# A first norm's rows loaded late, and a weight ring of 44 rows in place of 42

## The chip, the cores and the metric

The kernel runs on one core of a Trainium2 chip. The metric is the device time of one execution in microseconds (us). Engines are TensorE (PE in the profile; PEld is its weight load), VectorE (DVE), ScalarE (ACT), GpSimd (POOL) and SyncE (SP), which here issues nearly all DMA transfers.

## The reference

One decoder layer over 256 tokens of width 1024, all in float32:

```python
h = token_mixer(x, w_in, g_sb, g_dil, w_out, rel_bias)   # 8 stick-breaking and 8 dilated heads of 64
x = layer_norm(ALPHA * x + h, ln1_g, ln1_b)
h = grouped_moe(x, w_router, b_router, w_gate, w_up, w_down)
x = layer_norm(ALPHA * x + h, ln2_g, ln2_b)

# grouped_moe: 16 experts in 4 groups; each token picks one group, in it its top 2
for e in range(16):
    hid = silu(t @ w_gate[e]) * (t @ w_up[e])
    y = y + gate_dense[:, e:e+1] * (hid @ w_down[e])      # each w is 1024 x 1024
```

The expert weights are 16 x 3 x 4 MB, 201 MB, and each is used once.

## The kernel before

**The ring.** Each expert matrix is cut into 8 rows of 128 x 1024 floats (512 KB); `seq` lists the 384 rows in the order of use: gate, up and down of expert 0, then of expert 1, and so on. SBUF holds them in slots: `slot(i)` with i below `BIG` = 8 has room for 4 rows, the others for 2. `SMALL` slots of two rows (8 and 9) come from the base pool, which is there from the start, `LATE` of them (10, 11, 12) from a pool that is opened when attention is over. That makes a ring of 42 rows. Three more places take two rows each once and are not refilled: `fourth`, the slot `YS` (which afterwards is `ys2`, the experts' outputs and the gathered tokens), and the slot `OT` (attention's output before, and afterwards `acc`, the sum that the last norm reads). `lead` says which of the first 48 rows go where, `todo` is the list of the others in pairs.

**Refills.** When the last row of a slot has been multiplied, `taken` calls `load_next`, which takes the next pairs of `todo` into the slot (L236; `load_rows` splits a load where the rows go on in another matrix). The loads are issued by SP in program order, so a load that waits for its slot holds up those behind it. Slots 0 to 5 hold attention's input weights first, 6 and 7 the output projection. The last matrix, expert 15's down, is loaded by columns (L209). In expert 6 some slots are not refilled at once: they are `held` for a branch that recomputes experts with too many tokens, and refilled behind it, in expert 7.

**The experts.** They go in pairs; `pairs()` writes TensorE's order out by hand. Per expert: 16 rows of gate and up (L258), the activation (ACT L716, DVE L721), transposes (L723), 8 rows of down (L733). In between stand the gather of the next pair's tokens (L639, copied by ACT into `ys2[:, 1]`, then L648) and the spread of the last pair's outputs into `acc` (L670, L672), whose first is at row 2 of expert 2. The order on the other engines is the scheduler's.

**The first norm.** `xs` holds the normalised tokens without gain and bias. `ln1` holds gain and bias of the first norm as rows on all 128 partitions: loaded and broadcast at the start by `ln_rows` (L263, L264), the bias multiplied by ALPHA (L300). `residual()` is called when expert 0's down is done and writes ALPHA * (xs * gain + bias) into `acc`, with DVE (L679) and POOL (L680).

Of the kernel before, what the change touches and what calls it, by code (L numbers as in the profile page):

```python
# [13 lines left out]
F32 = mybir.dt.float32  # L14
I32 = mybir.dt.int32
AF = mybir.ActivationFunctionType
ALU = mybir.AluOpType
AX = mybir.AxisListType

D = 1024  # L20
T = 256
NT = T // 128
# [11 lines left out]
ALPHA = 2.0 ** 0.25  # L34
# [39 lines left out]

BIG = 8
W_IN = 6
SMALL, LATE = 2, 3
LATER = 40
CHUNKS = ((0, 512, 2), (512, 768, 4), (768, 1024, 2))
BANKS = {"mm": 3, "z": 2, "tr": 1, "om": 2}  # L80
SPARE = 6
# [3 lines left out]
def trunk(ctx: ExitStack, tc: tile.TileContext, x, w_in, g_sb, g_dil, w_out, ln1_g, ln1_b, ln2_g, ln2_b,  # L85
          rel_bias, w_router, b_router, w_gate, w_up, w_down, cst_d, rou_d, att_d, out):
    nc = tc.nc
# [4 lines left out]
    def pool(stack, name, bufs=1, **kw):  # L92
        return stack.enter_context(tc.tile_pool(name=name, bufs=bufs, reuse_waits="tile", **kw))

    base = pool(ctx, "base")
# [3 lines left out]
    def bank(name):  # L99
        return ps.tile([128, 512], F32, name=name, bufs=BANKS[name])  # L100
# [7 lines left out]
    OT, YS = BIG + SMALL + LATE, BIG + SMALL + LATE + 1  # L108
# [4 lines left out]
    def slot(i):  # L113
        p = base if i < BIG + SMALL or i == OT else late[0]
        return p.tile([128, room(i), D], F32, name=f"s{i}")

    def load_win(i, col, parts=(4, 4), between={}):
        src = w_in[:, col:col + 512].rearrange("(j p) f -> p j f", j=8)
        w = slot(i).rearrange("p a b -> p (a b)").rearrange("p (j f) -> p j f", j=8)
        j = 0  # L120
        for n in parts:
            if j in between:
                between[j]()
            nc.sync.dma_start(w[:, j:j + n], src[:, j:j + n])
            j += n
        return lambda j: w[:, j]
# [8 lines left out]
    xs = base.tile([128, NT, D], F32, name="xs")  # L135
# [13 lines left out]
    eps_rms = cst[:, C_EPS:C_EPS + 1]  # L149
    eps_ln = cst[:, C_EPS + 1:C_EPS + 2]  # L150
    ln_col = base.tile([128, 2, 8], F32, name="ln_col")
    ln1 = base.tile([128, 2, D], F32, name="ln1")
    pos1 = base.tile([128, NT, E], F32, name="pos1")
    gate = base.tile([128, NT, E], F32, name="gate")
    gate_ov = base.tile([128, NT, E], F32, name="gate_ov")
# [28 lines left out]
    def gathered(xp):  # L184
        xg = by_model()
        for j in range(8):
# [3 lines left out]

    seq = [(e, m, j) for e in range(E) for m in range(3) for j in range(8)]
    lead = {BIG: (0, 2), BIG + 1: (2, 4), BIG + 2: (4, 6), None: (6, 8), BIG + 3: (8, 10), BIG + 4: (10, 12),
            0: (12, 16), 1: (16, 20), YS: (20, 22), OT: (22, 24),
            **{i: (4 * i + 16, 4 * i + 20) for i in range(2, BIG)}}
    todo = [seq[n:n + 2] for n in range(48, len(seq), 2)]

    todo[-4:] = [[(E - 1, 2, q)] for q in range(4)]
    order = []
# [49 lines left out]
    def taken(row, refill=True):  # L248
        i = ring.pop(row)[1]
        if refill and i is not None and i < OT:  # L250
            load_next(i)
        return i

    def widened(p, row, xg, i):
        w = ring[row][0].rearrange("p (q c r) -> p c q r", c=2, r=4)
        j = row[2]
        for c in range(2):
            nc.tensor.matmul(p[c * CAP:(c + 1) * CAP], xg[:, j, i * CAP:(i + 1) * CAP], w[:, c],  # L258
                             start=j == 0, stop=j == 7)

    def ln_rows(dst, g, b):
        for i, v in enumerate((g, b)):
            nc.gpsimd.dma_start(dst[0:1, i], v)  # L263
            nc.gpsimd.partition_broadcast(dst[:, i], dst[0:1, i])  # L264


    with ExitStack() as mix:
# [11 lines left out]
        with ExitStack() as att:  # L279
# [16 lines left out]
            nc.sync.dma_start(ln_col[:, 0], ln1_g.rearrange("o (p j) -> (o p) j", j=8))  # L296
            nc.sync.dma_start(ln_col[:, 1], ln1_b.rearrange("o (p j) -> (o p) j", j=8))
            nc.sync.dma_start(rou, rou_d)
            ln_rows(ln1, ln1_g, ln1_b)
            nc.vector.tensor_scalar(ln1[:, 1], ln1[:, 1], ALPHA, None, op0=ALU.mult)  # L300
            c_vd, c_qd, c_kd = [load_win(i, c) for i, c in ((3, 2560), (4, 1536), (5, 2048))]
            wo = []
            for i in range(W_IN, BIG):
# [160 lines left out]
        for i, w in enumerate((wg, wr)):  # L464
            nc.vector.tensor_tensor(w, wr, gT[:, HG * (i + 1):HG * (i + 2)][:, :, None].to_broadcast([128, 8, E]),
                                    op=ALU.mult)
# [24 lines left out]
        for t in range(NT):  # L491
# [32 lines left out]
            if t == NT - 1:  # L524
# [41 lines left out]
                                           op0=ALU.is_ge, op1=ALU.mult)  # L566
# [3 lines left out]
                                           op0=ALU.is_equal, op1=ALU.mult)  # L570
# [10 lines left out]
            with tc.high_priority(offset=-LATER):  # L581
                if not t:
# [6 lines left out]
                                               op0=ALU.is_gt, op1=ALU.mult)  # L589
        xg = gathered(xp)  # L590
        with tc.high_priority(offset=-LATER):
            pp = bank("om")
            for t in range(NT):
                i = nc.tensor.matmul(pp[:, 0:E], ones, hots[:, t], start=t == 0, stop=t == NT - 1)
# [20 lines left out]
    acc = ys2 = last_silu = most = None  # L615
# [3 lines left out]
    def strips(v, c):  # L619
        return v.rearrange("p (h c f) -> p c h f", c=2, f=128)[:, c]  # L620

    def eighths(p):
        return p.rearrange("p (h f) -> p h f", f=128)
# [44 lines left out]
    def spread(pair, t, c):  # L668
# [2 lines left out]
        a = acc[:, t, c * 512:(c + 1) * 512]  # L671
        nc.vector.tensor_tensor(a, a, p, op=ALU.add)  # L672

    def residual():

        nonlocal acc
        acc = slot(OT)
        for t in range(NT):
            nc.vector.scalar_tensor_tensor(acc[:, t], xs[:, t], ALPHA, ln1[:, 0], op0=ALU.mult, op1=ALU.mult)  # L679
            nc.gpsimd.tensor_tensor(acc[:, t], acc[:, t], ln1[:, 1], op=ALU.add)  # L680


    def settle(t):
# [11 lines left out]
    def expert(e, xg, others):  # L695

        nonlocal last_silu, ys2
        i = e % 2

        def other(*place):  # L700
            for f in others.pop(place, ()):
                f()

        gu = []
        for m in range(2):
            p = gate0 if e == m == 0 else bank("mm")
            for j in range(8 if e == m == 0 else 0, 8):
                other("gu"[m], j)
                widened(p, (e, m, j), xg, i)
                hold = e == SPARE and m == 0 and j < 6  # L710
                s = taken((e, m, j), not hold)
                if hold and s is not None:
                    held.append(s)
            gu.append(p)
        h = wk.tile([128, 512], F32, name="h", bufs=1)
        last_silu = nc.scalar.activation(h, gu[0], AF.Silu)  # L716
        other("t", 0)
        hT = wk.tile([128, 4, 2, CAP], F32, name="hT", bufs=2)
        for rs, p in ((range(0, 2), bank("mm")), (range(2, 4), bank("om" if e < E - 2 else "tr"))):
            a, b = (v.rearrange("p (q r) -> p q r", r=4)[:, :, rs[0]:rs[0] + 2] for v in (h, gu[1]))  # L720
            nc.vector.tensor_tensor(a, a, b, op=ALU.mult)  # L721
            for r in rs:
                nc.tensor.transpose(p[:, r * 128:(r + 1) * 128], h[:, r::4], ident)  # L723
            nc.scalar.copy(hT[:, rs[0]:rs[0] + 2].rearrange("p r c s -> p (r c s)"),  # L724
                           p[:, rs[0] * 128:rs[0] * 128 + 256])
        other("t", 1)
        if e < E - 1:
            y = bank("tr")
            for j in range(8):
                other("d", j)  # L730
                w = ring[e, 2, j][0]
                for c in range(2):
                    nc.tensor.matmul(y[c * CAP:(c + 1) * CAP], hT[:, j % 4, j // 4], w[:, c * 512:(c + 1) * 512],  # L733
                                     start=j == 0, stop=j == 7)
                taken((e, 2, j))
            if e == 0:
                ys2 = slot(YS)
                residual()
            for c in range(2):
                nc.any.tensor_copy(ys2[i * CAP:(i + 1) * CAP, 0, c * 512:(c + 1) * 512], y[c * CAP:(c + 1) * CAP])  # L740
        assert not others, others
        return hT
# [75 lines left out]
    for n, (lo, hi, _) in enumerate(CHUNKS):  # L818
        y = bank("mm")[:, 0:(hi - lo) // 2]
        for j in range(8):  # L820
            for c in range(2):
                i = nc.tensor.matmul(eighths(y[c * CAP:(c + 1) * CAP]), hT[:, j % 4, j // 4],  # L822
                                     strips(ring["columns", lo, j], c), start=j == 0, stop=j == 7)
# [13 lines left out]
    for t, c in ((0, 0), (1, 1), (0, 1), (1, 0)):  # L837
        s, g, b, o = (strips(v, c) for v in (acc[:, t], ln2[:, 0], ln2[:, 1], out[toks[t]]))
# [4 lines left out]
        for h in ((slice(0, 2), slice(2, 4)) if t else (slice(0, 4),)):  # L843
# [3 lines left out]
            else:  # L847
                i = nc.vector.scalar_tensor_tensor(s[:, h], f[:, h], mv[:, 0:1], g[:, h],
                                                   op0=ALU.subtract, op1=ALU.mult)
# [64 lines left out]
```

## Time and profile before

| what | value |
|---|---|
| median of 3 runs | 610.55 us (608.6 to 611.08) |
| profiled execution: its time, its span | 608.12 us, 606.5 us |
| TensorE busy; VectorE; ScalarE; GpSimd | 96%; 22%; 17%; 4% of the span |
| moved by DMA | 222.51 MB, mean 367 GB/s |
| queue 1 (SP) share of 16 DMA engines' time | 88.9% |

Busy shares are means over the span; stages differ. Attention takes about the first 125 us, routing the time to 166 us, the experts the rest, the last norm the final 17 us. Matmuls are pipelined and their ends are modelled, so a TensorE that is shown busy isn't at its peak.

### The profile page before, as it was taken

What the parts mean: (1) busy time and instruction counts of PE and PEld (TensorE: products, weight loads), DVE (VectorE), ACT (ScalarE), POOL (GpSimd) and SP (SyncE); (2) the same over time, 40 slices, a digit from 0 to 9 for tenths busy, and PEclk for the clock granted to TensorE, in tenths of its full rate; (3) what the DMA queues carried; (4) which work ended last, traced back from release to release, by engine and by line L of the source; (5) the groups of instructions that cost most, each with busy time, mean ns of one, the idle gap of its engine ahead of it and who ended that gap; (6) DMA issues with size and microseconds to landing.
All of it is one profiled execution on the core that took longest, in us unless ns stands there. A gap on an engine that the chain in (4) does not pass through costs nothing. (4 is left out here: it accounts for less than half of the span.)

```text
span 606.5 us, 6495 instructions
## 1 busy us (share of the span) xinstructions
PE 581.8 (96%) x2617; PEld 260.5 (43%) x2618; DVE 132.1 (22%) x397; ACT 105.5 (17%) x239; POOL 22.4 (4%) x31
## 2 busy tenths in 40 slices
PE   8999999999999999999999999999999998899993
PEld 5677577745933333333333333333333332233342
DVE  0066413233621131031021103102110310030005
ACT  2144414321301111111101110111011010101011
POOL 2100001000003000000000000000000000002002
PEclk9999999999899999999999999999999998999997
DMA  8999831487589999999999999999999999999992
GB/s 282 354 369 420 376 139 35 159 306 316 208 307 394 423 423 430 426 427 418 426 425 421 426 425 423 426 420 424 424 430 428 424 419 428 424 419 424 421 337 71
DMA packets 35874, 222.51 MB, mean 367 GB/s; under 512 B 4704, under 2 KB 9088, under 8 KB 18176
## 3 DMA queue, kind: packets, MB, share of 16 engines
q1 hardware_dynamic: 34608, 220.61, 88.9%
q0 software_dynamic: 544, 1.08, 0.9%
q10 hardware_dynamic: 688, 0.36, 0.3%
q8 instruction: 22, 0.36, 0.2%
q14 instruction: 12, 0.10, 0.0%
HBM read 220.98 MB, written 1.06 MB: 366 GB/s over the span
## 5 line engine op out<-in xcount | busy, mean ns | idle before, releaser
L258 PE MATMUL mm<-s,xg 128*64 128x512 f32 x1016 | 225.8, 597 | 7.0 <-DMA s<-in_w_gate_dram 4.0
L258 PEld LDWEIGHTS mm<-s,xg 128*64 128x64 f32 x1016 | 72.2, 138 | 155.8 <-issue 143.6
L733 PE MATMUL tr<-s,hT 128*64 128x512 f32 x480 | 108.1, 597 | 1.5 <-DMA s<-in_w_down_dram 1.3
L721 DVE TENSOR_TENSOR h<-h,mm 128x256 f32<-128x256 f32 x32 | 12.1, 418 | 255.7 <-PE mm L258 255.7
L733 PEld LDWEIGHTS tr<-s,hT 128*64 128x64 f32 x480 | 32.5, 136 | 69.3 <-issue 58.8
L337 PE MATMUL mm<-xT,s 128*128 128x256 f32 x256 | 61.0, 384 | 0.0
L337 PEld LDWEIGHTS mm<-xT,s 128*128 128x128 f32 x256 | 46.9, 190 | 8.4 <-issue 3.0
L740 ACT COPY s<-tr 64x512 f32<-64x512 f32 x30 | 17.4, 580 | 109.7 <-PE tr L733 109.2
L716 ACT ACTIVATE h<-mm 128x512 f32<-128x512 f32 x16 | 9.6, 597 | 136.8 <-PE mm L258 136.8
L330 PE MATMUL mm<-s,xT 128*128 128x512 f32 x64 | 29.6, 600 | 0.3 <-DMA s<-in_w_in_dram 0.3
L639 PE MATMUL z<-xs,pick 128*128 128x512 f32 x56 | 29.0, 606 | 0.0
L176 DVE TENSOR_SCALAR xg<-z,ln_col 128x128 f32<-128x128 f32 x56 | 18.5, 401 | 43.7 <-PE z L648 43.7
L670 PE MATMUL om<-s,back 128*128 128x512 f32 x56 | 27.3, 618 | 0.0
L672 DVE TENSOR_TENSOR s<-s,om 128x512 f32<-128x512 f32 x28 | 19.2, 687 | 33.8 <-PE om L670 33.6
L480 PE MATMUL mm<-s,s 128*128 128x512 f32 x48 | 23.0, 602 | 0.0
L670 PEld LDWEIGHTS om<-s,back 128*128 128x128 f32 x56 | 9.0, 188 | 18.2 <-DVE s L672 9.2
L724 ACT COPY hT<-mm 128x256 f32<-128x256 f32 x16 | 6.0, 373 | 61.5 <-PE mm L723 61.5
L330 PEld LDWEIGHTS mm<-s,xT 128*128 128x128 f32 x64 | 11.4, 190 | 12.1 <-issue 10.6
L263 POOL DMA_DIRECT2D s<-in_ln_g_dram x1 | 0.7, 710 | 354.3 <-DMA s<-in_w_up_dram 354.3
L661 DVE TENSOR_SCALAR wp<-cst,pos,gate 128x64 f32<-128x64 f32 x36 | 8.8, 307 | 13.6 <-PE z L663 8.3
L665 ACT COPY back<-z 128x256 f32<-128x256 f32 x8 | 3.0, 373 | 50.0 <-PE z L663 50.0
L639 PEld LDWEIGHTS z<-xs,pick 128*128 128x128 f32 x56 | 8.7, 193 | 6.6 <-issue 6.6
(172 smaller groups left out, 373.5 us busy)
## 6 DMA issues: line engine op xcount, KB each, us to landing
s<-in_w_up_dram SPq DMA_DIRECT2D x17, 2048.0 KB, 11.0
s<-in_w_down_dram SPq DMA_DIRECT2D x17, 2048.0 KB, 21.7
s<-in_w_gate_dram SPq DMA_DIRECT2D x16, 2048.0 KB, 18.3
s<-in_w_gate_dram SPq DMA_DIRECT2D x31, 1024.0 KB, 24.7
s<-in_w_up_dram SPq DMA_DIRECT2D x30, 1024.0 KB, 23.4
s<-in_w_down_dram SPq DMA_DIRECT2D x26, 1024.0 KB, 24.6
s<-in_w_in_dram SPq DMA_DIRECT2D x10, 1024.0 KB, 8.0
s<-in_w_out_dram SPq DMA_DIRECT2D x4, 1024.0 KB, 14.9
```

The lines of the kernel that those rows point to most:

```text
L176: return nc.vector.tensor_scalar(dst, src, ln_col[:, 0, j:j + 1], ln_col[:, 1, j:j + 1], op0=ALU.mult, op1=ALU.add)
L258: nc.tensor.matmul(p[c * CAP:(c + 1) * CAP], xg[:, j, i * CAP:(i + 1) * CAP], w[:, c], start=j == 0, stop=j == 7)
L330: nc.tensor.matmul(p, xT[:, j, t * 128:(t + 1) * 128], w(j), start=j == 0, stop=j == 7)
L337: nc.tensor.matmul(p[:, 0:T], w(j)[:, i * 128:(i + 1) * 128], xT[:, j], start=j == 0, stop=j == 7)
L480: nc.tensor.matmul(pr[t][n][:, 0:hi - lo], oT[:, k, t * 128:(t + 1) * 128], wo[k // 4][:, k % 4, lo:hi], start=k == 0, stop=k == 7)
L639: nc.tensor.matmul(self.xp[c], self.pick[t], xs[:, t, c * 512:(c + 1) * 512], start=t == 0, stop=t == NT - 1)
L670: nc.tensor.matmul(p, backs[pair][:, toks[t]], ys2[:, 0, c * 512:(c + 1) * 512], start=True, stop=True)
L672: nc.vector.tensor_tensor(a, a, p, op=ALU.add)
L716: last_silu = nc.scalar.activation(h, gu[0], AF.Silu)
L721: nc.vector.tensor_tensor(a, a, b, op=ALU.mult)
L733: nc.tensor.matmul(y[c * CAP:(c + 1) * CAP], hT[:, j % 4, j // 4], w[:, c * 512:(c + 1) * 512], start=j == 0, stop=j == 7)
L740: nc.any.tensor_copy(ys2[i * CAP:(i + 1) * CAP, 0, c * 512:(c + 1) * 512], y[c * CAP:(c + 1) * CAP])
```

## The change

`ln1` is gone, and with it its load, broadcast and multiply at the start. `residual()` loads the gain into row 0 of `ys2[:, 1]` and the bias into row 0 of `acc[:, 1]`, each of which is free at that time, broadcasts both there and computes the sum in place with four DVE operations. The 8 KB per partition go to one more slot of two rows: slots 8, 9 and 10 are now in the base pool, 11, 12 and 13 in the late one, `OT` is slot 14 and `YS` slot 15. In `lead` the special slots take rows 16 to 19, slot 1 takes 20 to 23 (it had 16 to 19), and slot 13 takes 48 and 49. `todo` starts at row 50. In expert 6 all slots that end in the gate rows are held, where rows 6 and 7 were left out.

```diff
-SMALL, LATE = 2, 3
+SMALL, LATE = 3, 3
...
-    ln1 = base.tile([128, 2, D], F32, name="ln1")
...
-            0: (12, 16), 1: (16, 20), YS: (20, 22), OT: (22, 24),
-            **{i: (4 * i + 16, 4 * i + 20) for i in range(2, BIG)}}
-    todo = [seq[n:n + 2] for n in range(48, len(seq), 2)]
+            0: (12, 16), YS: (16, 18), OT: (18, 20), **{i: (4 * i + 16, 4 * i + 20) for i in range(1, BIG)},
+            BIG + 5: (48, 50)}
+    todo = [seq[n:n + 2] for n in range(50, len(seq), 2)]
...
-            ln_rows(ln1, ln1_g, ln1_b)
-            nc.vector.tensor_scalar(ln1[:, 1], ln1[:, 1], ALPHA, None, op0=ALU.mult)
...
     def residual():
         nonlocal acc
         acc = slot(OT)
-        for t in range(NT):
-            nc.vector.scalar_tensor_tensor(acc[:, t], xs[:, t], ALPHA, ln1[:, 0], op0=ALU.mult, op1=ALU.mult)
-            nc.gpsimd.tensor_tensor(acc[:, t], acc[:, t], ln1[:, 1], op=ALU.add)
+        g, b = ys2[:, 1], acc[:, 1]
+        for dst, v in ((g, ln1_g), (b, ln1_b)):
+            nc.gpsimd.dma_start(dst[0:1], v)
+        for dst in (g, b):
+            nc.gpsimd.partition_broadcast(dst, dst[0:1])
+        for t, dst in enumerate((acc[:, 0], g)):
+            nc.vector.scalar_tensor_tensor(dst, xs[:, t], ALPHA, g, op0=ALU.mult, op1=ALU.mult)
+            nc.vector.scalar_tensor_tensor(acc[:, t], b, ALPHA, dst, op0=ALU.mult, op1=ALU.add)
...
-                hold = e == SPARE and m == 0 and j < 6
+                hold = e == SPARE and m == 0
```

## Rows read from the trace of the kernel before

**Rows 1.** Page, the span in 40 slices: busy tenths of PE, and GB/s moved

```profile
PE   8999999999999999999999999999999998899993
...
GB/s 282 354 369 420 376 139 35 159 306 316 208 307 394 423 423 430 426 427 418 426 425 421 426 425 423 426 420 424 424 430 428 424 419 428 424 419 424 421 337 71
```

**Rows 2.** Chain of waits in order of time: start, length, what

```profile
442.27 34.66 DMA s<-in_w_gate_dram
...
496.82 24.64 DMA s<-in_w_up_dram
```

**Rows 3.** Waits of PE, 430 to 600 us: total, times, longest

```profile
PE mm L258 <- DMA s<-in_w_gate_dram: 4.0, 3, 2.4
PE mm L258 <- DMA s<-in_w_up_dram: 2.2, 2, 1.2
PE tr L733 <- DMA s<-in_w_down_dram: 1.3, 1, 1.3
```

**Rows 4.** Timeline of PE in the last experts: start, length, instructions [idle before]

```profile
537.34 1.94 PE L258 MATMUL mm<-s,xg 128*64 128x512 f32 x8 [0.76 <-DMA s<-in_w_gate_dram]
...
543.03 12.24 PE L258 MATMUL mm<-s,xg 128*64 128x512 f32 x56
...
584.67 0.51 PE L723 MATMUL mm<-cst,h 128*128 128x128 f32 x2 [0.59 <-DVE h L721]
```

**Rows 5.** Windows: length, busy of each engine, PEclk, DMA share, GB/s

```profile
164.00:169.90 5.90, 5.90 (x27) 3.58 (x28) 3.13 (x10) 0.00 (x0) 0.00 (x0) 1.00 0.12 22
169.90:188.00 18.10, 17.70 (x84) 6.20 (x82) 2.63 (x10) 1.63 (x4) 0.00 (x0) 1.00 0.99 390
188.00:194.00 6.00, 6.00 (x30) 2.01 (x28) 2.36 (x2) 1.16 (x2) 3.49 (x2) 1.00 0.99 395
194.00:196.00 2.00, 2.00 (x12) 0.72 (x10) 0.00 (x0) 0.00 (x0) 2.00 (x1) 1.00 0.86 328
196.00:200.00 4.00, 4.00 (x22) 1.29 (x18) 0.00 (x0) 0.60 (x1) 0.07 (x1) 1.00 0.97 401
240.00:300.00 60.00, 60.00 (x267) 20.88 (x264) 8.18 (x22) 7.52 (x15) 0.00 (x0) 1.00 1.01 424
```

**Rows 6.** Timeline of SP, merged; the x1 lines from narrower windows

```profile
168.47 7.19 SPq L236 DMA_DIRECT2D s<-in_w_gate_dram  x4
177.06 9.02 SPq L236 DMA_DIRECT2D s<-in_w_up_dram  x3
...
185.75 0.33 SPq L236 DMA_DIRECT2D s<-in_w_up_dram  x1
...
192.62 0.33 SPq L236 DMA_DIRECT2D s<-in_w_down_dram  x1
```

**Rows 7.** Timeline of DVE, 186 to 206 us, all its lines

```profile
189.19 2.36 DVE L679 SCALAR_TENSOR_TENSOR s<-xs,ln 128x1024 f32<-128x1024 f32 x2 [6.98 <-PE tr L733]
202.99 0.75 DVE L721 TENSOR_TENSOR h<-h,mm 128x256 f32<-128x256 f32 x2 [11.44 <-PE mm L258]
```

**Rows 8.** Page, DMA queues: packets, MB, share of 16 engines' span

```profile
q8 instruction: 22, 0.36, 0.2%
```

**Rows 9.** Timeline of POOL: the broadcasts, and the issue before the second

```profile
11.74 2.48 POOL L264 PARTITION_BROADCAST ln<-ln  x2 [8.75 <-issue]
...
551.15 0.49 POOL L263 DMA_DIRECT2D s<-in_ln_b_dram  x1
557.91 2.48 POOL L264 PARTITION_BROADCAST s<-s  x2 [6.27 <-issue]
```

**Rows 10.** Single lines L300, L679, L680: ns min/median/max, first to last start

```profile
L300 DVE TENSOR_SCALAR ln<-ln x1: 694/694/694, 14.3 to 14.3; 128x1024 f32<-128x1024 f32 x1
...
L679 DVE SCALAR_TENSOR_TENSOR s<-xs,ln x2: 1219/1222/1225, 189.2 to 190.3; 128x1024 f32<-128x1024 f32 x2
...
L680 POOL TENSOR_TENSOR s<-s,ln x2: 2352/2802/3253, 190.5 to 193.7; 128x1024 f32<-128x1024 f32 x2
```

**Rows 11.** Timeline of PE: expert 0's down projection

```profile
182.06 7.09 PE L733 MATMUL tr<-s,hT 128*64 128x512 f32 x32 [0.18 <-ACT hT L724]
```

## The prediction

> **What bounds the kernel now.** I read the slices first. TensorE (PE) is busy in nearly every slice, and from about 180 us to the last slices the bytes moved stand at 420 to 430 GB/s [rows 1]. Two resources are therefore full at once, and the question is which of them ends last. The chain of waits answers it: back from the end from 442 us on it consists mostly of DMA pieces of 20 to 35 us with TensorE pieces between [rows 2]. TensorE's own waits confirm it: after 430 us it waits 4.0, 2.2 and 1.3 us for expert weights, 7.5 us together [rows 3]. Before 430 us it eats from a ring that was filled during attention; TensorE uses it up faster than the stream refills it, and then it stands still now and then. The last such stand is at 537.34; from there it runs without one until the activations of the last expert at 584.67 [rows 4].
>
> So the end goes by the weight stream: when it becomes continuous, and how much is still to be moved then. In 240 to 300 us it moves 424 GB/s [rows 5]. Two rows are 2 x 512 KB = 1.049 MB, or 2.47 us of stream.
>
> **The sum is made against** the profiled execution, span 606.5 us, which took 608.12 us by its own time; the median of the three runs shown is 610.55, 2.4 above it. I carry differences from the one to the other.
>
> **Two rows more in the ring.** Slot 10 moves to the base pool and is loaded with slots 8 and 9, before anything waits; a new slot 13 takes rows 48 and 49. About 1.05 MB more is in SBUF before the experts start. The transfer lies ahead of a hole: the slices around 80 to 105 us move 139 and 35 GB/s [rows 1]. It costs nothing there; without that hole it would cost the 2.47 us that it saves. Gain: 2.47 us, if all later refills come when they did.
>
> **They do not all come then.** Refills are issued when the last row of a slot is consumed. Slots 8 to 12 and 0 still end at rows 1, 3, 5, 9, 11 and 15. Slot 1 ended at row 19 and now ends at row 23, because rows 16 to 19 went to the two special slots, which are not refilled. Its refill (the third transfer of the group that starts at 177.06) is issued at 185.75 [rows 6]. Row 23 is the last of expert 0's down projection: VectorE's residual, which waits for exactly that row now, starts at 189.19 [rows 7]. The refill comes 3.4 us later.
>
> Is the queue empty by then? Issued before it, from 168.47 on, are five transfers of 1.05 MB and one of 2.1 MB, 7.34 MB. Until 169.9 about 0.13 MB were moved, and from 169.9 to 188.0 18.1 us x 390 GB/s = 7.06 MB [rows 5]. What remains, 0.15 MB, is through at 188.4. A transfer issued into an empty queue starts to move about 1.3 us later (168.47, moving by 169.9), so slot 1 moves from 190.5: a hole of 2.1 us. Its 2.1 MB end at 190.5 + 4.95 = 195.4. Slot 2 is issued at 192.62 in both kernels [rows 6] and can't move before 193.9. Before, slot 1 was through at 188.4 + 4.95 = 193.4 and the stream had a small hole of its own (328 GB/s in 194 to 196 [rows 5]). So slot 2 now starts at 195.4 where it started at 193.9: 1.5 us later, with two rows more behind it. After that nothing is short: issues run ahead of the bytes. Net gain of the stream: 2.47 - 1.5 = 1.0 us.
>
> Bounds: if the hole is paid in full, 2.47 - 2.1 = 0.4 us. On the other side, the stream lost (424 - 395) x 6 / 424 + (424 - 328) x 2 / 424 + (424 - 401) x 4 / 424 = 1.1 us between 188 and 200 [rows 5]; part of that are fetches of instructions, each of which holds one of the 16 engines for about a microsecond (22 packets on queue 8, 0.2% of 16 spans, 0.9 us each [rows 8]). If these fall into the new hole, up to 1.1 us is not lost a second time: 2.1 us.
>
> **Larger transfers.** With the list starting at row 50, rows of 4-row slots start at a multiple of four, so most refills are one transfer of 2 MB, where before about every second was split in two. Rows then arrive four at a time. The place where this matters is behind TensorE's last stand. There gate rows 0 to 3 of expert 14 arrive at about 537.2. The transfer with up rows 4 to 7 ends 12 rows later, 12 x 1.236 = 14.8 us, at 552.0. TensorE gets there after 12 rows of 0.86 us (56 matmuls, 14 rows, in 12.24 us) and a 3.8 us spread [rows 4], at 551.5: a wait of about 0.6 us, where before the first two of these rows came 2.47 us earlier. So TensorE gains 1.0 - 0.6 = 0.4, the stream 1.0; the tail needs both. I take 0.7, the middle.
>
> **The rows of the first norm.** Removed at the front: two 4 KB transfers, two broadcasts of 2.48 us together [rows 9] and a VectorE multiply of 0.69 us [rows 10] at 14 us, for which nobody waits; VectorE's first work after it comes later. Worth nothing. Removed at 190: the two POOL additions.
>
> Added: the special slot for outputs is free after down row 1 (182.06 + 2 x 0.89 = 183.9 [rows 11]), that for the sum after row 3, which is slot 1's old point, 185.75 [rows 6]. POOL issues the two transfers, the second done at 186.25. From the end of such an issue to the broadcast 6.27 us passed in the late stretch, 8.75 in the first [rows 9]. Broadcasts start at 192.5 to 195.0, the first ends 1.3 us later, and four VectorE operations of 1.22 [rows 10] follow: done between 198.7 and 201.2. Behind them on VectorE stands expert 1's product at 202.99 [rows 7], and TensorE waits for that. Cover: 1.8 to 4.3 us. ScalarE's copies into the same slot follow only after the product. Cost 0; without the cover, each microsecond would stop TensorE.
>
> The idle time before each first broadcast is what the Trainium skill describes (GPSIMD Engine Reference, Instruction dispatch): the first call of freshly loaded code pays about 6 us. By its 5.95 the chain would be done near 198.4, an estimate; the first stretch's 8.75 is longer, and I keep the rows.
>
> The two POOL additions took 3.25 and 2.35 us, the longer one started while VectorE was at work [rows 7, 10]. The Trainium skill (SBUF — State Buffer, SBUF: two separate sides) says that the two engines lock each other out of a port pair for a whole instruction. By that rule the second broadcast and the first VectorE operation could not overlap: 1.2 us more on the chain, still under 202.99.
>
> **Held slots.** Expert 6 now keeps back slots 11, 12 and 0 instead of 0 and 1: eight rows either way, of a ring larger by two. The stream showed no dip in those slices [rows 1]. Cost 0.
>
> **Rivals.** *Full gain* (chance 0.2): the hole is hidden by what was lost there anyway and the larger transfers cost nothing; 2.1 to 2.5 us, 608.3. For it: the losses of 1.1 us in just that stretch. *No gain* (0.22): the hole costs 2.1 and the coarser arrivals the rest; 0 to 0.3 us slower, 610.7. For it: the queue at 188 is nearly empty in the rows. That would also be how the change fails to do what it says: a larger ring that gives back at slot 1 what it took in. *Slower* (0.11): the rows are late. VectorE's four operations hold the product of expert 1, TensorE stops at 204, and so do the refills. TensorE has 7.5 us of waits to give away, so it decides only if VectorE is done after 202.99 + 7.5 = 210.5, 9 us beyond my upper end. If POOL's start took three times its longest row (26 us), VectorE would end at 218.5, 8 us beyond that point: 618. Against it: both rows of such a start.
>
> **How the numbers follow.** Forecast (0.47): gain 0.7 us, own range 0.4 to 2.1; span 605.8, profiled time 607.4, median 609.9. The runs shown spread from 608.6 to 611.08, and half a per cent, 3.05 us, is about what can be told from no change. Faster by over that needs more than the whole 1.05 MB; only the full gain with fewer fetches on the slowest engine gets there: 0.12. Slower: the late rows, 0.11. Same: 0.77. The range runs from the full gain and the lower half of the spread, 606.8, to no gain and its upper half, with a little of the slower case: 612.0.
>
> **What would show it.** The profile after should show: TensorE's waits for weights after 430 us still near 7 us in sum; VectorE's four operations ending before 203 and the product still at 203.0; a hole in the stream at 188 to 191 and slot 1's refill issued at 189.2; 424 GB/s from 196 on; the last stand of TensorE at about 536.5. The prediction is wrong if the product starts after 204, if the stream shows no hole (then the full gain), or if TensorE's waits sum to far more than 8 us.

## The result and the profile after

The changed kernel takes 606.01 us (median of 4 runs, 605.49 to 606.92) where the kernel before takes 610.82 in the same comparison: ratio 0.9937, interval 0.9919 to 0.9956, or 3.85 us with bounds of 2.7 and 4.9 (the two medians by themselves lie 4.8 us apart, inside these bounds). In a second comparison the ratio was 0.9937 again (0.9922 to 0.9951). The forecast was a gain of 0.7 us, 609.9, with a range down to 606.8. The direction holds, the time lies just below the range, and the size is off by a factor of more than five.

The page after. First the bytes moved in 40 slices, then the DMA issues of the expert weights by size (count, KB each, median us to landing):

```profile
GB/s 278 374 392 420 411 143 35 147 295 342 210 246 367 430 426 423 430 427 420 428 428 428 421 425 422 427 429 427 425 419 431 425 423 428 428 425 419 421 363 79
...
s<-in_w_up_dram SPq DMA_DIRECT2D x22, 2048.0 KB, 12.7
s<-in_w_down_dram SPq DMA_DIRECT2D x22, 2048.0 KB, 17.3
s<-in_w_gate_dram SPq DMA_DIRECT2D x20, 2048.0 KB, 29.6
s<-in_w_gate_dram SPq DMA_DIRECT2D x23, 1024.0 KB, 27.1
s<-in_w_up_dram SPq DMA_DIRECT2D x20, 1024.0 KB, 21.0
s<-in_w_down_dram SPq DMA_DIRECT2D x16, 1024.0 KB, 18.9
```

There are 64 transfers of 2 MB and 59 of 1 MB. The kernel before has 50 and 87:

```profile
s<-in_w_up_dram SPq DMA_DIRECT2D x17, 2048.0 KB, 11.0
s<-in_w_down_dram SPq DMA_DIRECT2D x17, 2048.0 KB, 21.7
s<-in_w_gate_dram SPq DMA_DIRECT2D x16, 2048.0 KB, 18.3
s<-in_w_gate_dram SPq DMA_DIRECT2D x31, 1024.0 KB, 24.7
s<-in_w_up_dram SPq DMA_DIRECT2D x30, 1024.0 KB, 23.4
s<-in_w_down_dram SPq DMA_DIRECT2D x26, 1024.0 KB, 24.6
```

So 14 pairs of 1 MB have become one transfer each.

The windows of the stretch in question (length, busy of each engine, PEclk, DMA share, GB/s), which answer to [rows 5]:

```profile
169.90:188.00 18.10, 17.70 (x84) 6.18 (x82) 2.63 (x10) 1.63 (x4) 1.03 (x2) 1.00 0.97 368
188.00:194.00 6.00, 6.00 (x30) 2.00 (x28) 0.00 (x0) 1.16 (x2) 0.27 (x1) 1.00 0.77 280
194.00:196.00 2.00, 2.00 (x12) 0.71 (x10) 0.93 (x1) 0.00 (x0) 2.00 (x2) 1.00 0.99 426
196.00:200.00 4.00, 4.00 (x20) 1.28 (x18) 3.87 (x4) 0.60 (x1) 0.21 (x1) 1.00 0.98 420
240.00:300.00 60.00, 60.00 (x268) 20.99 (x266) 8.19 (x22) 7.51 (x15) 0.00 (x0) 1.00 1.01 426
```

The hole is there: 280 GB/s in 188 to 194 is (424 - 280) x 6 / 424 = 2.0 us lost, where 2.1 were worked out. Behind it the stream is full at once. And the steady rate is 426 where it was 424.

Timeline of SP, narrowed to the refills of slots 0 and 1, for [rows 6]: slot 0 before, then slots 0 and 1 after.

```profile
180.49 0.33 SPq L236 DMA_DIRECT2D s<-in_w_up_dram  x1
...
181.67 0.33 SPq L235 DMA_DIRECT2D s<-in_w_up_dram  x1
190.37 0.33 SPq L235 DMA_DIRECT2D s<-in_w_down_dram  x1
```

Before, slot 1's stood at 185.75: 5.3 us between the two, now 8.7, the 3.4 us of the working.

Timeline of POOL around both loads of norm rows, and of VectorE behind the first (start, length, [idle before <- what ended it]), for [rows 9] and [rows 7]:

```profile
185.78 0.52 POOL L677 DMA_DIRECT2D s<-in_ln_g_dram  x1 [72.26 <-DMA s<-in_w_up_dram]
187.20 0.51 POOL L677 DMA_DIRECT2D s<-in_ln_b_dram  x1 [0.90 <-PE tr L735]
193.73 2.48 POOL L679 PARTITION_BROADCAST s<-s  x2 [6.03 <-issue]
...
551.81 2.49 POOL L263 PARTITION_BROADCAST s<-s  x2 [4.42 <-DMA s<-in_ln_g_dram]
```

```profile
195.07 2.08 DVE L681 SCALAR_TENSOR_TENSOR s<-xs,s 128x1024 f32<-128x1024 f32 x1 [11.67 <-POOL s L679]
197.24 1.23 DVE L682 SCALAR_TENSOR_TENSOR s<-s 128x1024 f32<-128x1024 f32 x1
198.38 1.22 DVE L681 SCALAR_TENSOR_TENSOR s<-xs,s 128x1024 f32<-128x1024 f32 x1
199.63 1.22 DVE L682 SCALAR_TENSOR_TENSOR s<-s,s 128x1024 f32<-128x1024 f32 x1
204.18 0.75 DVE L723 TENSOR_TENSOR h<-h,mm 128x256 f32<-128x256 f32 x2 [3.32 <-PE mm L257]
```

VectorE is done at 200.9, 3.3 us before expert 1's product, which waited for TensorE alone. The product starts at 204.18, after the 204 that the prediction named as a sign of being wrong; but the experts start 1.2 us later in this trace (below), and counted from there the product stands where it stood before. POOL stood 6.03 us before its first broadcast. Before the second norm's broadcast it waited for nothing beyond the landing, where in the kernel before, with POOL's additions in between, 6.27 us passed. That fits code that is loaded once and still there, which no run tests.

TensorE's waits for weights, 430 to 600 us, and its last stands, for [rows 3] and [rows 4]:

```profile
PE mm L257 <- DMA s<-in_w_up_dram: 3.2, 2, 3.0
PE mm L257 <- DMA s<-in_w_gate_dram: 1.2, 3, 0.5
```

```profile
534.81 1.94 PE L257 MATMUL mm<-s,xg 128*64 128x512 f32 x8 [0.26 <-DMA s<-in_w_gate_dram]
...
549.48 3.65 PE L257 MATMUL mm<-s,xg 128*64 128x512 f32 x16 [0.18 <-DMA s<-in_w_up_dram]
...
582.53 0.51 PE L725 MATMUL mm<-cst,h 128*128 128x128 f32 x2 [0.59 <-DVE h L723]
```

It waits 4.4 us, not 7.5. The coarser arrival shows at the place named, up row 4 of expert 14, at 549.48, with 0.18 us of idle time instead of 0.6.

**What the two spans hide.** They differ by only 2.6 us, 606.5 and 603.9. The first matmul of the experts' weights starts earlier in the trace of the kernel before (timelines of PE, before and after):

```profile
166.49 5.37 PE L258 MATMUL mm<-s,xg 128*64 128x512 f32 x24
```

```profile
167.68 5.37 PE L257 MATMUL mm<-s,xg 128*64 128x512 f32 x24
```

That start lies between 166.5 and 169.8 in the twelve traces of this study, and between 166.5 and 169.8 in the three traces of the kernel before alone. From the start of the experts to the end it is 440.0 us before and 436.2 after, 3.8 us, which is the measured ratio. For all traces, worked out from the landing records of the DMA: the last transfer of up weights of expert 15 lands in 16 parts, one per DMA engine, and TensorE can go on after the last of them. (At its last stand before, 370.85 us after the experts' start, the parts of the gate transfer that it waited for had landed from 365.73 to 370.71.)

```
from the experts' first matmul, us      first of 16   last of 16   apart   end
before, three traces                    410.3         415.4        5.1     440.0
                                        410.3         415.0        4.7     440.1
                                        410.7         416.2        5.6     440.8
changed, two traces                     408.3         411.6        3.3     436.2
                                        408.3         411.9        3.6     436.4
hole42: before, slot 1 late             411.8         415.2        3.4     440.1
no_hole: changed, slot 1 early          407.2         411.6        4.4     436.2
all_split: changed, 1 MB transfers      412.3         415.8        3.5     439.7
split42: before, 1 MB transfers         413.8         419.0        5.3     443.0
norm_alone: before, late norm rows      410.4         413.7        3.2     437.9
wide: changed, more 2 MB transfers      407.9         411.2        3.3     436.6
chain_late: changed, late residual      408.8         412.1        3.3     437.0
```

### The profile page after: what moved, and what is told of

The parts are those of the page before. It is cut to its first block, busy times and chain, and to the rows that moved or that the text cites. A ratio compares the mean times of both kernels' runs of the same rounds, so it can differ in the third digit from the quotient of the medians.

```text
span 603.9 us, 6479 instructions
## 1 busy us (share of the span) xinstructions
PE 583.0 (97%) x2617; PEld 262.2 (43%) x2618; DVE 134.8 (22%) x398; ACT 105.5 (17%) x239; POOL 16.6 (3%) x29
## 4 chain that ended last, share of the span: by engine, by line
PE 59%; DMA 35%; DVE 3%; ACT 2%; issue 1%; POOL 0%; POOLq 0%; SPq 0%; ACTq 0%; DVEq 0%
DMA s<-in_w_up_dram 31%; PE mm L257 19%; PE tr L735 9%; PE mm L334 6%; PE mm L327 5%; PE mm L477 4%; DMA s<-in_w_gate_dram 3%; PE z L636 2%; PE om L667 2%; PE mm L171 1%; PE mm L824 1%; PE om L433 1%; PE z L477 1%; PE z L350 1%; PE tr L357 1%; DVE s L373 1%
## 5 line engine op out<-in xcount | busy, mean ns | idle before, releaser
L357 PE MATMUL tr<-cst,s 128*128 128x128 f32 x48 | 8.9, 283 | 2.4 <-ACT s L376 1.1
```

The costliest lines, as they stand in the source:

```text
L357: nc.tensor.transpose(p[:, b * 128:(b + 1) * 128], a[:, b * 128:(b + 1) * 128], ident)
```

## The experiments

Two theories stood against each other. By the prediction, the late refill of slot 1 costs 1.5 us and the larger transfers are worth nothing or a little less. By the new one, the hole costs the slowest of the 16 DMA engines nothing, and every transfer saved is worth 0.06 us: in the trace of the kernel before, late in the stream, a transfer of 1 MB lands 2.48 us after the one ahead of it and one of 2 MB 4.90, so two small ones take 0.06 longer.

**The changed kernel again.**

> The changed kernel once more, beside the others on one chip. Both theories: 0.994 of the kernel before, as measured. Its trace gives a second sample of how far the 16 landings of the last up transfer lie apart (3.3 us in the first trace, 5.1 in the kernel before).

Measured 0.9937 (0.9922 to 0.9951), and the 16 landings lie 3.6 us apart. The gain repeats.

**Slot 1 early again (no_hole).**

```diff
-            0: (12, 16), YS: (16, 18), OT: (18, 20), **{i: (4 * i + 16, 4 * i + 20) for i in range(1, BIG)},
+            0: (12, 16), 1: (16, 20), YS: (20, 22), OT: (22, 24), **{i: (4 * i + 16, 4 * i + 20) for i in range(2, BIG)},
```

> The changed kernel with rows 16 to 19 in slot 1 again and the special slots at rows 20 to 23, so that slot 1 is refilled after row 19; the residual's rows come 3.4 us later. Theory of the prediction (slot 1's late refill costs 1.5 us net): 1.5 us faster than the changed kernel, ratio to before 0.991. Theory of the stream (the hole is paid in full, some 2.0 us): 2.0 us faster, 0.990. Rival (the hole only takes up waits of slow engines that come back later): no faster than the changed kernel, 0.994. The residual ends near 204.3, about when expert 1's product is due at 204.2; a stop of TensorE of up to 1.5 us there should cost nothing.

Measured 0.9948 (0.9930 to 0.9965): not faster than the changed kernel. The 0.990 and the 0.991 of the two theories of a costly hole lie outside the interval. Its windows show why the mean rate gains little either:

```profile
188.00:194.00 6.00, 6.00 (x31) 2.00 (x29) 0.00 (x0) 1.16 (x2) 1.02 (x2) 1.00 1.00 416
194.00:196.00 2.00, 2.00 (x12) 0.71 (x10) 0.00 (x0) 0.00 (x0) 0.00 (x0) 1.00 0.75 240
196.00:200.00 4.00, 4.00 (x20) 1.29 (x18) 0.52 (x1) 0.60 (x1) 1.85 (x2) 1.00 0.97 369
```

The hole at 188 is closed and a smaller one opens at 194, behind slot 1, because slot 2's refill is issued at its old time: 0.1 + 0.9 + 0.5 = 1.5 us lost against 2.0. So only 0.5 us of stream came back, not 2.0. A hole paid in full would by that give 0.9929, just below the interval: the time by itself refutes the two forecasts made for this run, but hardly that a hole is paid. The landings say more: the first of the 16 comes 1.1 us earlier than in the changed kernel (407.2 against 408.3), the last one not (411.6 and 411.6).

**All transfers of 1 MB (all_split).**

```diff
-            if b == len(rows) or rows[b] != (e, m, j + b - a) or e == E - 1 and b - a == 2:
+            if b == len(rows) or rows[b] != (e, m, j + b - a) or b - a == 2:
```

> The changed kernel with every refill in transfers of two rows (1 MB), none of four. Theory of the prediction (larger transfers cost TensorE 0.6 us of waiting and the stream nothing): 0 to 0.6 us faster than the changed kernel, 0.993. Theory of the stream (each cut in two costs 0.06 us, 1.0 MB lands every 2.48 us, 2.1 MB every 4.90): 64 cuts more, 3.5 us slower than the changed kernel, ratio to before about 1.000.

Measured 0.9991 (0.9980 to 1.0003), 3.3 us slower than the changed kernel. After the first fills 56 transfers are cut, so 0.06 us each. The steady rate falls with it:

```profile
240.00:300.00 60.00, 60.00 (x266) 20.90 (x264) 8.20 (x22) 7.51 (x15) 0.00 (x0) 1.00 1.01 421
```

2.1 MB take 4.98 us at 421 GB/s and 4.92 at 426, where two in three of the bytes still come in 2 MB transfers.

**The late rows alone, ring of 42 (norm_alone).** `SMALL`, `lead`, `todo` and the held slots of the kernel before, `residual()` of the changed one.

> The kernel before with the new residual alone: rows loaded late into the special slots, ring of 42 rows and its order as before, the 8 KB left empty. Both theories: 1.000, within 0.2%: the chain of POOL and VectorE lies beside the stream. Rival (the load, broadcast and multiply at the start were in the way of something, or TensorE is stopped at expert 1 and pays for it): off 1.000 by more than 0.3%.

Measured 1.0013 (0.9998 to 1.0028). The late norm rows alone give nothing. As in no_hole, the slots come free 3.4 us later than in the changed kernel, so VectorE's chain is done only at 205.9, and expert 1's product behind it starts at 205.76, over 1 us later than it was due. Its one trace, 437.9 us from the experts' start, comes from the fastest of its 12 runs.

**The two rows alone (split42).** The kernel before with the cut of all_split, so that it differs from that one by the rest of the change only: the two rows, the late refill of slot 1, the held slots and the residual.

> The kernel before with every load in transfers of two rows. Beside the changed kernel with all loads so split (0.9991 of the kernel before) it differs by the two rows more and the residual alone, with no difference in the size of transfers. Theory: two rows are 2.47 us of stream, so this one lies 0.40% above that, at 1.003; by its own cuts (some 42 in the stream, 0.055 us each, 2.3 us) 1.004. Rival (the two rows are given back at slot 1's late refill, and the gain came from the larger transfers): as the split changed kernel, 0.999 to 1.000.

Measured 1.0037 (1.0012 to 1.0063). Against 0.9991 (each set against the kernel before in its own comparison) that is 0.46%, 2.8 us for the two rows with the hole and the late norm rows, where 2.47 were worked out for the rows alone; the traces differ by 3.3 us at the end. The rival's 0.999 to 1.000 is outside. Cutting 42 transfers cost the kernel before 2.3 us, cutting 56 the changed one 3.3: the 14 transfers between them are worth about 1.0 us by that, 0.8 by the price of 0.06.

**More large transfers (wide).** The six two-row slots become two of four rows and two of two:

```diff
-SMALL, LATE = 3, 3
+SMALL, LATE = 2, 2
...
-        return 4 if i < BIG else 2
+        return 4 if i <= BIG or i == BIG + 2 else 2
...
-    lead = {BIG: (0, 2), BIG + 1: (2, 4), BIG + 2: (4, 6), None: (6, 8), BIG + 3: (8, 10), BIG + 4: (10, 12),
+    lead = {BIG + 1: (0, 2), BIG: (2, 6), None: (6, 8), BIG + 2: (8, 12),
...
-            BIG + 5: (48, 50)}
+            BIG + 3: (48, 50)}
```

> The changed kernel with four of its six two-row slots joined to two four-row slots: ring of 44 rows as before, some 14 transfers of 2 MB in place of 28 of 1 MB. Theory of the stream (0.055 us for each transfer saved): 0.8 us faster than the changed kernel, ratio 0.992. Rival (rows arrive four at a time, TensorE waits more): no faster, 0.994 or above.

Measured 0.9933 (0.9908 to 0.9957): inconclusive. Both its own forecast and the changed kernel's 0.9937 lie inside. The last landing comes 0.5 us earlier in its trace, the end does not.

**The kernel before, two more traces (before_2, before_3).**

> The kernel before once more, for its trace. Theory: the first trace of it had an early start of the experts (168.47, where the traces of the changed kernels have 169.6 to 171.7) and landings that lay further apart at the end; a second one starts at 169.6 or later, and from that start to the last landing of the up weights it takes about 413 us, as the first, against 409.6 to 409.9 for the changed kernel.

> The same as the run before it, a third trace: 413 us from the start of the experts to the last landing of the up weights, if the difference of the two traces on record is the kernel's and not that execution's.

The experts start at 169.8 and 169.7. The expectations count from the first refill, 2.0 us later: by that the last up weights land after 413.1 and 414.3 us, against 413.4 in the first trace and 409.6 to 409.9 in the changed kernel. So the early start was that execution's, and the longer stream is the kernel's.

**The hole alone (hole42).** Before's ring, with only this changed:

```diff
-            0: (12, 16), 1: (16, 20), YS: (20, 22), OT: (22, 24),
-            **{i: (4 * i + 16, 4 * i + 20) for i in range(2, BIG)}}
+            0: (12, 16), YS: (16, 18), OT: (18, 20), **{i: (4 * i + 16, 4 * i + 20) for i in range(1, BIG)}}
```

> The kernel before with rows 16 to 19 in the special slots and 20 to 23 in slot 1, as in the changed kernel, and nothing else: slot 1's refill 3.4 us later, ring of 42 rows, norm rows at the start. Theory of the prediction: the hole costs 1.5 us, ratio 1.0025. Theory of the slowest engine (TensorE waits for the last of 16 landings; the hole takes 1.1 us from the engines that are ahead and nothing from the one behind): 1.000, and in its trace the first of the 16 landings of the last up transfer comes about 1 us later after the experts' start than in the kernel before (410.3 to 410.7), the last one not (415.0 to 416.2).

Measured 0.9998 (0.9971 to 1.0025). The time alone only just reaches the 1.0025 of the prediction's theory; the trace separates them. The hole is as deep as in the changed kernel:

```profile
188.00:194.00 6.00, 6.00 (x30) 2.01 (x28) 1.09 (x1) 1.16 (x2) 5.57 (x2) 1.00 0.71 266
194.00:196.00 2.00, 2.00 (x12) 0.62 (x10) 0.00 (x0) 0.00 (x0) 0.00 (x0) 1.00 1.04 434
196.00:200.00 4.00, 4.00 (x22) 1.40 (x20) 0.00 (x0) 0.60 (x1) 0.00 (x0) 1.00 1.04 444
```

The first landing comes 1.1 to 1.5 us later than before (411.8), the last does not (415.2), and the end is 440.1, as before.

The landings show it at once behind the hole, too. The first transfer there, slot 2's, is issued 26.1 us after the experts' start in nine of the traces, as one of 2 MB. Its first part lands at 34.3 to 34.5 us in the four of them with the hole and at 32.9 to 33.4 in the five without. Its last part lands at 34.8 to 35.8 and at 34.6 to 36.2: no later for the hole.

**A late residual (chain_late).** Each broadcast four times, in place.

```diff
-        for dst in (g, b):
+        for dst in (g, g, g, g, b, b, b, b):
```

> The changed kernel with each of the two broadcasts made four times, in place: VectorE's four operations end near 207.3 in place of 200.9, expert 1's product, due at 204.2, comes 3.1 us late, and TensorE stops for that long. Theory (TensorE has 4 to 7 us of waits for weights to give away, and the queue of issued refills covers the stream): ratio to before as the changed kernel, 0.994, and TensorE's waits for weights after 430 us smaller by 3. Rival (a stop of TensorE there holds back refills and costs itself): 3.1 us slower, 0.999.

Measured 0.9947 (0.9923 to 0.9972). VectorE and TensorE behind it:

```profile
208.33 0.41 DVE L723 TENSOR_TENSOR h<-h,mm 128x256 f32<-128x256 f32 x1
208.66 1.22 DVE L682 SCALAR_TENSOR_TENSOR s<-s,s 128x1024 f32<-128x1024 f32 x1
209.79 0.41 DVE L723 TENSOR_TENSOR h<-h,mm 128x256 f32<-128x256 f32 x1
```

```profile
212.42 2.80 PE L735 MATMUL tr<-s,hT 128*64 128x512 f32 x12
```

In the first trace of the changed kernel expert 1's down projection stands here:

```profile
208.09 3.65 PE L735 MATMUL tr<-s,hT 128*64 128x512 f32 x16
```

The experts start 2.0 us later in the trace of chain_late, so it should begin at 210.1 and begins at 212.4. Of this stop of 2.3 us 0.7 is left at the end (437.0 against 436.3), no more than the three traces of the kernel before differ by (440.0 to 440.8). TensorE's waits for weights after 430 us are 3.0 us, against 4.4 and 6.0 in the two traces of the changed kernel. The 0.999 of the rival is outside.

## Why the prediction was wrong

*The bound was right.* The stream sets the end: cutting its transfers of 2 MB moves the last landing by 4.0 to 4.2 us (all_split against the changed kernel) and the end by 3.3 to 3.5.

*Two rows more: 2.47 us, right as far as measured.* With all transfers of 1 MB, and with the hole, the held slots and the late norm rows, it is 2.8 us, within the noise of the two intervals. The held slots were not measured alone.

*The late refill of slot 1: the first step that failed.* The hole came where and as deep as worked out, 2.0 us, and the first part of slot 2's transfer landed 1.0 to 1.6 us later (two traces after, three before), where 1.5 were forecast. But "net gain of the stream: 2.47 - 1.5 = 1.0 us" took the stream for one queue. It is 16, and TensorE waits for the last of them. The hole takes time only from engines that are ahead: in hole42 the first of 16 loses 1.1 to 1.5 us up to the end, the last nothing. The bound on the other side had this (fetches that fall into the hole are not paid twice), and of the two ends the wrong one was taken as nearer.

The landings also show how an engine comes to be last. In the trace of before, first and last part of a transfer lie 2.1 us apart from 35 to 111 us after the experts' start, and then in steps 2.6, 3.4, 4.0 and 5.0: an engine that was held up stays behind. In 25 of the 26 steps of over 0.3 us in the twelve traces, a fetch of instructions (0.9 to 1.1 us on one engine, 14 or 15 of them in 400 us) had begun 2.1 to 6.3 us before the late landing. That makes the fetches the likely cause, though steps of up to 1.7 us are longer than one of them, and no run changed them.

The hole lets the last ones catch up. It delays the mean of the 16 by 0.6 to 1.0 us (hole42 at the last up transfer: 413.5 against 412.4, 412.5 and 412.9) and brings the last one nearer to it by 0.9 to 1.6. At the end first and last lie 3.3 to 3.6 us apart in the six traces with the hole and 4.4 to 5.6 in five of the six without. The sixth, norm_alone with 3.2, had 3.1 already at slot 2's transfer, where those with the hole have 0.5 to 1.6, and no such step after it; why it had none is open.

*Larger transfers: the second step that failed, in sign.* It was costed as a wait of TensorE of 0.6 us, and the saving in the stream at nothing, though the trace of before holds both sizes. The wait came with 0.2 us of idle time. Each transfer saved is worth 0.06 us: 14 of them 0.8 us. The Trainium skill (SBUF — State Buffer, The DMA setup-cost knee) says to coalesce into the largest transfers, as each carries a fixed cost of about 2 us. The direction holds here; in a queue that is never empty the cost is 0.06 us, measured; that the rest of it lies beside the transfers ahead is a reading that no run tests.

*The sum with these terms*: 2.47 (worked out) + 0.8 - 0 = 3.3 us, or 3.6 with the 2.8 of split42, both within 2.7 to 4.9. What lies between them and 3.85, if anything, isn't settled.

*The norm rows: right.* 200.9 lies between 198.7 and 201.2, the cover was 3.3 us, the cost nothing that was measured: norm_alone, where the chain ends later and without cover, has 1.0013, with 1.000 inside its interval. POOL's start took 6.03 us, near the late row. The first VectorE operation took 2.08 us where 1.22 is usual, while the second broadcast ran. That fits the lock that the Trainium skill describes (SBUF — State Buffer, SBUF: two separate sides): 0.9 us, under the cover as said.

*The slower rival* fails because the rows were in time. Its other half, that TensorE's later waits take up a stop, chain_late bears out: they took up 1.6 of 2.3 us, and the 0.7 that is left can't be told from the scatter of the traces.

*The chances.* Faster by over half a per cent got 0.12, as the sum of the gain and the fetches; with the transfers costed and the hole at nothing it would have been the likeliest. The choice of 0.7, a middle between two numbers that were both too low, had no row behind it.

## What to carry to other kernels

Where one stream of loads sets the end, the bytes that are already in memory when it becomes continuous are worth their time at the stream's rate, and each transfer that is merged into another has a price of its own: read it off before, as the difference between two small landings and one large. A hole early in the stream is to be costed at the DMA engine that lands last, not at the mean rate. And two profiled spans are compared from a common event, here the experts' start, which moved by 3 us between executions of the same kernel.

## What the runs showed of the hardware that was not expected

The 16 parts of one transfer land 3.2 to 5.6 us apart near the end of the stream, and grow apart in steps that stay, nearly each behind a fetch of instructions. A hole of 2.0 us brought them back to 0.5 to 1.6 us. Transfers of 2 MB move at 426 GB/s in the mix of the changed kernel, transfers of 1 MB at 421, in the same full queue. The start of the experts varies from 166.5 to 169.8 us in three executions of one kernel.
